# Block 2's shifts and scales as 512-column products with loads of their own and partial sums through DRAM

## The chip, the cores and the metric

The kernel runs on one core of a Trainium2 chip. The time is the device time of one execution in microseconds (us): before the change 2770.35 us, the median of 3 runs (2768.22 to 2776.49). One execution was also taken with the hardware profiler; all rows below are from it. The engines are PE (TensorE; PEld is its weight load), ACT (ScalarE), DVE (VectorE), POOL (GpSimd), and SP (SyncE), which only issues DMAs here.

## The reference, cut to what matters

Two transformer blocks with two layers each run one after the other. Block 1 has 512 rows of width 1024. In each of its layers one projection feeds four kinds of attention: "fox" (causal softmax), stick-breaking, latent (causal softmax again, with low-rank queries and keys), and attention over a memory; a gate and an output projection end the layer. Block 2 modulates its rows by shifts and scales that depend on two condition vectors alone, and so on nothing that block 1 computes:

```python
def adaln(cond, w_mod_l, b_mod_l, n_chunks):
    m = jax.nn.silu(cond) @ w_mod_l[:, :n_chunks * D_MODEL] + b_mod_l[:n_chunks * D_MODEL]
    return jnp.split(m, n_chunks, axis=-1)

def modulate(x, shift, scale):
    return layer_norm(x) * (1 + scale) + shift
# in layer l of block 2, for the latents and for the context:
sh1, sc1, g1, sh2, sc2, g2 = [m[:, None, :] for m in adaln(c, w_mod[l], b_mod[l], N_MOD)]
ctx_mod = adaln(c_ctx, w_mod[l], b_mod[l], 2 if last else N_MOD)
```

The weights of one layer are 1024 rows by 6144 columns of float32, 24 MB, and there are two layers. The left operand has two rows (c and c_ctx).

## The kernel before, in words

`block1` (L600) computes one layer of block 1. In its gaps it runs a generator, `adaln` (L415), which computes the shifts and scales of the same layer of block 2: layer 0's beside layer 0 of block 1, and layer 1's beside layer 1. The generator is put into the list `bg` after the fox attention, and `tick` advances it by one `yield`. There are ticks after the stick-breaking projections, in every second step of stick-breaking attention (L674), after the latent projections, around the latent attention and in the gate's loop; `drain` runs what is left.

One step of `adaln` makes 512 of the 6144 columns. It fetches the 1024 weight rows of these columns in four loads of 512 KB (`wraw`, L318: two times 128 rows by 512 columns). The loads go into the three buffers `w` of a ring that all weights of the two blocks share, and they are issued by SP, whose queue runs in order. For each group of 128 rows, four products of 128 columns each go to the four column tiles of the PE array (32 columns wide), the same left operand `cT` in each, and accumulate over the eight groups in one PSUM tile `pj` (two buffers, which all projections share). So a step is 32 products, and a layer is 12 steps and 48 loads. A float32 product is two PE instructions. DVE adds the bias into the row tile `mr`; when all steps are done, `mr` goes to DRAM (`mod_d`) and comes back in two layouts, to be transposed into `modc` and `modw`.

The names that the change touches: `wraw` and `pj` as above; `copy` (L125) moves a tile on ACT or DVE, taking turns when it isn't told which; `small(..., "ty", bufs=4)` is a tile of 128 by 512 with four buffers, used all over block 1; `causal_attn` (L483) is the fox and the latent attention, eight iterations each; `full_attn` (L505) the memory attention. The order of instructions on each engine is set by a list scheduler at build time, not by the order of the code; at run time each engine takes its list in order.

## Time and profile before

| what | value |
|---|---|
| time of the runs | 2770.35 us (2768.22 to 2776.49) |
| the profiled execution | 2777.7 us, its span 2775.9 us |
| PE busy | 2406.4 us, 87% of the span |
| PE busy from 90 to 400 us (layer 0 of block 1) | 278.84 of 310 us |
| PE busy from 480 to 790 us (layer 1 of block 1) | 278.14 of 310 us |
| loads of `w_mod` | 96 of 512 KB, issued from 90.8 to 747.9 us |

A group's row in the profile gives the engine, the line of the kernel, the operation, the tiles it writes and reads (out<-in), the shape, the count, and busy time; a row of the timeline gives start, length and the same, and in brackets the idle time before it and what ended it. L151 is the helper that issues every product, so products are told apart by their tiles: `pj<-w,cT` are those of `adaln`.

### The profile page before, as it was taken

The page shows a single profiled execution, that of the slowest core. Times are in us where ns is not written, and L with a number is a line of the kernel's source. Part 1 is how long each engine was busy: PE and PEld are TensorE (multiplying, and loading weights), DVE is VectorE, ACT ScalarE, POOL GpSimd, SP SyncE. Part 2 cuts the span into 40 slices and gives each one's busy share as a digit, 9 for nine tenths or more (in the row PEclk, how much of TensorE's full clock was granted, in tenths as well). Part 3 has the DMA queues.
Part 4 walks back from the last instruction along what each step waited for, and adds up shares of the span by engine and source line. Part 5 has one row for each costly group of instructions (what it writes and reads, how often), then busy time and mean ns, then how long its engine had stood idle before and what let it go on. Part 6 is the DMA issues. An engine that isn't in the chain of part 4 may idle for free.

```text
span 2775.9 us, 39464 instructions
## 1 busy us (share of the span) xinstructions
PE 2406.4 (87%) x16255; PEld 1439.1 (52%) x16255; DVE 1224.7 (44%) x2367; ACT 801.2 (29%) x1522; POOL 508.8 (18%) x389
## 2 busy tenths in 40 slices
PE   6988889988998887995999999995798959988887
PEld 5765667655677665774333333334576733333323
DVE  4423554423666977866010101028778661112213
ACT  3353332363334434742101010103337420000001
POOL 3101222011233234042001010104322420000001
PEclk9999999999999997997999999998999969999998
DMA  5353562354444124035899999982221459999996
GB/s 179 116 169 120 164 182 84 107 184 141 133 134 153 61 99 128 8 131 212 355 393 349 419 341 420 340 337 100 68 68 30 160 207 410 421 420 421 421 421 233
DMA packets 216746, 613.17 MB, mean 221 GB/s; under 512 B 37592, under 2 KB 110830, under 8 KB 170486
## 3 DMA queue, kind: packets, MB, share of 16 engines
q1 hardware_dynamic: 207142, 576.74, 55.8%
q0 software_dynamic: 5440, 20.45, 2.6%
q10 hardware_dynamic: 3984, 13.45, 1.2%
q8 instruction: 128, 2.10, 0.3%
q14 instruction: 52, 0.43, 0.0%
HBM read 581.92 MB, written 28.67 MB: 220 GB/s over the span
## 4 chain that ended last, share of the span: by engine, by line
PE 35%; DVE 13%; DMA 11%; issue 8%; ACT 2%; POOL 2%; DVEq 0%; POOLq 0%; ACTq 0%; SPq 0%
PE pm L151 20%; PE pj L151 5%; PE pa L151 5%; DMA w<-in_w_up_dram 4%; DMA w<-in_w_gate_dram 4%; DVE acc L865 3%; DMA w<-in_w_down_dram 2%; PE pt L151 2%; PE pt L160 1%; DVE wl L331 1%; PE ptm L160 1%; DVE s L245 1%; POOL lnst L249 1%; ACT P L471 1%; DVE ng L468 1%
## 5 line engine op out<-in xcount | busy, mean ns | idle before, releaser
L151 PE MATMUL pm<-w,q 128*64 128x512 f32 (+1 forms) x1600 | 359.5, 597 | 40.3 <-DMA w<-in_w_up_dram 27.6
L151 PE MATMUL pm<-w,xT 128*32 128x512 f32 x3072 | 338.7, 599 | 0.0
L151 PEld LDWEIGHTS pm<-w,q 128*64 128x64 f32 x1600 | 122.6, 141 | 265.3 <-issue 200.5
L329 ACT ACTIVATE wh<-w 128x1024 fp32r<-128x1024 f32 (+2 forms) x154 | 161.3, 1050 | 317.2 <-PE pj L151 106.7
L331 POOL TENSOR_TENSOR wl<-w,wh 128x1024 fp32r<-128x1024 f32 (+1 forms) x57 | 143.5, 2520 | 464.0 <-ACT wh L329 448.0
L151 PE MATMUL pj<-hTh,wh 128*128 128x512 f32 x512 | 215.8, 422 | 13.3 <-ACT ty L301 7.2
L151 PEld LDWEIGHTS pm<-w,xT 128*32 128x32 f32 x3072 | 104.4, 111 | 228.1 <-issue 223.6
L151 PE MATMUL pj<-hTl,wh 128*128 128x512 f32 x512 | 207.7, 406 | 0.0
L151 PE MATMUL pj<-hTh,wl 128*128 128x512 f32 x512 | 206.1, 406 | 0.0
L151 PE MATMUL pm<-w,hid 128*32 128x512 f32 x1536 | 178.5, 593 | 0.0
L331 DVE TENSOR_TENSOR wl<-w,wh 128x1024 fp32r<-128x1024 f32 (+2 forms) x97 | 132.4, 1366 | 102.7 <-ACT wh L329 102.1
L1276 DVE TENSOR_TENSOR q<-pm,q 128x512 f32<-128x512 f32 x24 | 16.6, 692 | 285.6 <-PE pm L151 285.6
L160 PE MATMUL pt<-ident,P 128*128 128x128 f32 x712 | 121.2, 290 | 13.0 <-DVE mx L133 4.8
L151 PE MATMUL pa<-wh,hTh 128*128 128x512 f32 x256 | 106.3, 416 | 22.4 <-DVE ty L963 15.1
L1276 DVE TENSOR_TENSOR ty<-pm,ty 128x512 f32<-128x512 f32 x16 | 11.1, 691 | 256.4 <-PE pm L151 256.4
L151 PEld LDWEIGHTS pj<-hTh,wh 128*128 128x128 f32 x512 | 100.7, 197 | 40.5 <-issue 8.9
L1180 POOL DMA_INDIRECT q<-rowsl,idx x16 | 15.4, 960 | 563.0 <-PE ptm L160 432.7
L151 PEld LDWEIGHTS pj<-hTh,wl 128*128 128x128 f32 x512 | 99.5, 194 | 26.0 <-issue 3.3
L151 PEld LDWEIGHTS pj<-hTl,wh 128*128 128x128 f32 x512 | 100.2, 196 | 24.7 <-issue 4.2
L468 DVE TENSOR_REDUCE ng<-pa 128x1 f32<-128x513 f32 (+5 forms) x124 | 93.4, 756 | 35.1 <-PE pa L151 33.1
L151 PEld LDWEIGHTS pm<-w,hid 128*32 128x32 f32 x1536 | 50.4, 110 | 112.5 <-issue 110.7
L865 DVE SCALAR_TENSOR_TENSOR acc<-glu,vec,acc 128x512 f32<-128x512 f32 x120 | 108.6, 946 | 0.1
(447 smaller groups left out, 4465.3 us busy)
## 6 DMA issues: line engine op xcount, KB each, us to landing
w<-in_w_gate_dram SPq DMA_DIRECT2D x128, 1024.0 KB
w<-in_w_up_dram SPq DMA_DIRECT2D x127, 1024.0 KB
w<-in_w_down_dram SPq DMA_DIRECT2D x118, 1024.0 KB
w<-in_w_mod_dram SPq DMA_DIRECT2D x96, 512.0 KB
w<-in_w_in_dram SPq DMA_DIRECT2D x94, 512.0 KB
w<-in_w_out_dram SPq DMA_DIRECT2D x40, 512.0 KB
w<-in_w_down_dram SPq DMA_DIRECT2D x16, 512.0 KB
z<-q ACTq DMA_DIRECT2D x8, 512.0 KB
```

The source lines that it names most:

```text
L151: return T.matmul(o, l, r, start=start, stop=stop_, skip_group_check=True, **kw)
L160: T.transpose(o, i, ident[: i.shape[0], : i.shape[0]])
L245: pin(V.bn_stats(s6[:, c, :], x[:, c * w:c * w + w]))
L249: pin(G.tensor_tensor(out=rs, in0=ve, in1=mhalf[:, :n], op=OP.pow))
L329: A.activation(hi, w, AF.Copy)
L331: (lo_eng or (G if lot[0] % 3 == 0 else V)).tensor_tensor(out=lo, in0=w, in1=hi.bitcast(F32), op=OP.subtract)
L468: V.tensor_reduce(ng, S_[:, :, lo:hi], axis=AX, op=OP.max, negate=True)
L471: A.activation(P[:, i, lo:hi], S_[:, i, lo:hi], AF.Exp, bias=ng[:, i:i + 1], accum_out=su[:, i:i + 1])
L865: V.scalar_tensor_tensor(acc[:, c, :n], glu[:, c, tap:tap + n], w, acc[:, c, :n], op0=OP.mult, op1=OP.add)
L1180: pin(G.indirect_dma_start(out=r, out_offset=None, in_=s["rows"][:], in_offset=bass.IndirectOffsetOnAxis(ap=s["idx"][:, i:i + 1], axis=0)) ...
L1276: V.tensor_tensor(out=x, in0=up[b][h], in1=x, op=OP.mult)
```

## The change

A step now makes half of the sum for 512 columns: it takes 512 of the 1024 rows as four groups of 128, and gives each group to one of the four column tiles, as one product of 512 columns. Each column tile has a group of its own, nothing is accumulated, and the four partial sums stand in partitions 0, 32, 64 and 96 of `pj`. A step has 4 products and 2 loads, and a layer has 24 steps. The loads go into two buffers `wm` of the generator's own pool, and a step issues those of the next one, so the weights of the other projections have the ring to themselves. `copy` brings the whole tile of partial sums to a `ty` tile, a DMA issued by ACT writes it to DRAM (`part_d`), and when all steps are done, the partial sums come back as a tile of 96 by 8 by 128, DVE adds the eight, and the bias. Ticks are added: in every step of stick-breaking attention, and in every iteration of `causal_attn`.

```diff
     def adaln(l, pool):
-        mr = pool.tile([128, 12, 128], F32, tag="mr", name="mr")
...
-        for u in range(12):
+        part_d = dr.tile([2, 128, 6 * D], F32, name=f"adp{l}")
+        def wm():
+            return pool.tile([128, 1024], F32, tag="wm", name="wm", bufs=2)
+        def load(n):
+            u, h = divmod(n, 2)
+            ws = []
+            for j in range(2):
+                w = wm().rearrange("p (k c) -> p k c", k=2)
+                nc.sync.dma_start(w, a["w_mod_2"][l, 512 * h + 256 * j:512 * h + 256 * j + 256,
+                                                  512 * u:512 * u + 512].rearrange("(k p) c -> p k c", p=128))
+                ws.append(w)
+            return ws
+        ws = load(0)
+        yield
+        for n in range(24):
+            u, h = divmod(n, 2)
             p = pj()
-            for kq in range(4):
-                w = wraw(a["w_mod_2"][l], 2 * kq, 2, 512 * u, 512)
-                for k in range(2):
-                    for g in range(4):
-                        mm(p[32 * g:32 * g + 32, :128], cT[:, 2 * kq + k, :], w[:, k, 128 * g:128 * g + 128],
-                           kq == 0 and k == 0, kq == 3 and k == 1, tile_position=(0, 32 * g))
-            V.tensor_tensor(out=mr[:, u, :], in0=p[:, :128], in1=mr[:, u, :], op=OP.add)
+            for g in range(4):
+                mm(p[32 * g:32 * g + 32, :], cT[:, 4 * h + g, :], ws[g // 2][:, g % 2, :], True, True,
+                   tile_position=(0, 32 * g))
+            if n < 23:
+                ws = load(n + 1)
+            y = small([128, S], "ty", bufs=4)
+            copy(y, p)
+            nc.scalar.dma_start(part_d[h, :, 512 * u:512 * u + 512], y)
             yield
-        for g in range(4):
-            nc.sync.dma_start(mod_d[l]..., mr[32 * g:32 * g + 2, :, :])
...
+        m8 = wm()[:96].rearrange("p (a b) -> p a b", b=128)
+        for h in range(2):
+            nc.sync.dma_start(m8[:, 4 * h:4 * h + 4, :], ...part_d[h]...)
+        m9 = wm()
...
+        for w_ in (4, 2, 1):
+            V.tensor_tensor(out=m8[:, :w_, :], in0=m8[:, :w_, :], in1=m8[:, w_:2 * w_, :], op=OP.add)
+        mraw = m9[:96, 128:256]
+        V.tensor_tensor(out=mraw, in0=m8[:, 0, :], in1=m9[:96, 0:128], op=OP.add)
+        nc.sync.dma_start(mod_d[l].rearrange("c (k p) -> (c k) p", p=128), mraw)
...
 # causal_attn, end of each iteration
+                tick(1)
 # stick-breaking attention
-                if j % 2 == 0:
-                    tick(1)
+                tick(1)
```

SP's queue beside stick-breaking attention and the latent projections of layer 0, before (`w` is a buffer of the shared ring; `wk` and `wq` are the latent up-projections' weights):

```order
L321 DMA w<-in_w_in_dram 128x4x256 x2
L321 DMA w<-in_w_mod_dram 128x2x512
L694 DMA P<-in_k_tabs_dram 128x1024
L321 DMA w<-in_w_mod_dram 128x2x512 x3
L749 DMA wk<-in_w_mla_kv_up_dram 128x4x64 x2
```

and now (`wm` are the two own buffers):

```order
L428 DMA wm<-in_w_mod_dram 128x2x512 x2
L321 DMA w<-in_w_in_dram 128x4x256 x2
L428 DMA wm<-in_w_mod_dram 128x2x512 x2
L773 DMA wk<-in_w_mla_kv_up_dram 128x4x64 x2
L428 DMA wm<-in_w_mod_dram 128x2x512 x16
L718 DMA P<-in_k_tabs_dram 128x1024
```

Sixteen loads of `wm`, those of eight steps, now stand behind each other, and the last two of them are those of the step that PE takes after the latent projections; `wk` has moved ahead of them.

PE in the latent attention of layer 0 (`pa<-q,q` are scores, `pt<-ident,P` transposes of the probabilities, `pt<-P,v` products with the values), before:

```order
L151 MATMUL pj<-w,cT 32x128 x8
L160 MATMUL pt<-ident,P 128x128 x4
L151 MATMUL pj<-w,cT 32x128 x16
L151 MATMUL pt<-P,v 64x128 x4
L151 MATMUL pa<-q_2193,q_2195 128x128
```

and now, at the same place:

```order
L160 MATMUL pt<-ident,P 128x128 x2
L151 MATMUL pj<-wm,cT 32x512 x2
L160 MATMUL pt<-ident,P 128x128 x2
L151 MATMUL pj<-wm,cT 32x512 x2
L151 MATMUL pt<-P,v 64x128 x4
L151 MATMUL pa<-q_1988,q_1990 128x128
```

The four products of a step mostly stand as two pairs, one for each load, with other work between; before, the products of one load were eight, and those of two or more loads often stood together.

ACT at the same place, before (`P,su<-pa,ng` are the exponentials):

```order
L471 ACTIVATE P,su_2403<-pa,ng_2401 128x512 x2
L329 ACTIVATE wh<-w 128x1024
L131 ACTIVATE P<-pt 128x512
L471 ACTIVATE P,su_2441<-pa,ng_2439 128x128 x2
L329 ACTIVATE wh<-w 128x1024
```

and now:

```order
L495 ACTIVATE P,su_2204<-pa,ng_2202 128x512 x2
L131 ACTIVATE ty<-pj 128x512
L445 DMA adp_1142<-ty 128x512
L131 ACTIVATE P<-pt 128x512
L495 ACTIVATE P,su_2254<-pa,ng_2252 128x128 x2
```

The casts of the gate's weights (`wh<-w`) have moved behind this place, and in each iteration a copy of partial sums and the issue of its DMA stand in ACT's list between the exponentials.

## Rows read from the trace of the kernel before

**Rows 1.** The page, part 1: busy time and share of the span.

```profile
PE 2406.4 (87%) x16255; PEld 1439.1 (52%) x16255; DVE 1224.7 (44%) x2367; ACT 801.2 (29%) x1522; POOL 508.8 (18%) x389
```

**Rows 2.** The chain of waits from 780 to 830 us: its earliest two pieces.

```profile
822.99 0.04 issue
823.03 7.05 PE pj L151 x58
```

**Rows 3.** PE's waits in 0 to 460, 171 to 232, 565 to 600, 460 to 860 us.

```profile
PE pj L151 <- DMA w<-in_w_mod_dram: 16.7, 12, 3.3
...
PE pj L151 <- DMA w<-in_w_mod_dram: 8.2, 7, 2.8
...
PE pj L151 <- DMA w<-in_w_mod_dram: 8.7, 7, 2.3
...
PE pj L151 <- DMA w<-in_w_mod_dram: 18.3, 13, 2.8
```

**Rows 4.** The timeline of PE: 32 instructions of `adaln`, and what starts behind them.

```profile
281.40 1.08 PE L151 MATMUL pj<-w,cT 128*32 128x128 f32 x32
282.41 0.91 PE L151 MATMUL pa<-q,q 96*128 96x384 f32 x2
```

**Rows 5.** The page, part 5: 512-column products in two and in four column tiles.

```profile
L151 PE MATMUL pm<-w,q 128*64 128x512 f32 (+1 forms) x1600 | 359.5, 597 | 40.3 <-DMA w<-in_w_up_dram 27.6
L151 PE MATMUL pm<-w,xT 128*32 128x512 f32 x3072 | 338.7, 599 | 0.0
```

**Rows 6.** The timeline of SP and PE: issues of loads, and the products that waited for them.

```profile
260.37 0.37 SPq L321 DMA_DIRECT2D w<-in_w_mod_dram  x1
...
264.92 0.64 PE L151 MATMUL pj<-w,cT 128*32 128x128 f32 x16 [3.20 <-DMA w<-in_w_mod_dram]
265.98 2.08 PE L151 MATMUL pj<-cqk,wk 128*128 128x512 f32 x2 [0.41 <-DVE mr L430]
...
270.10 1.02 PE L151 MATMUL pj<-cqk,wk 128*128 128x512 f32 x2
...
282.10 0.88 SPq L321 DMA_DIRECT2D w<-in_w_mod_dram  x2
...
286.30 0.64 PE L151 MATMUL pj<-w,cT 128*32 128x128 f32 x16 [1.22 <-DMA w<-in_w_mod_dram]
...
657.05 0.65 PE L151 MATMUL pj<-w,cT 128*32 128x128 f32 x16 [2.47 <-DMA w<-in_w_mod_dram]
658.11 2.08 PE L151 MATMUL pj<-cqk,wk 128*128 128x512 f32 x2 [0.41 <-DVE mr L430]
```

**Rows 7.** Windows: busy time of the engines, granted clock (PEclk), DMA share, GB/s.

```profile
180.00:190.00 10.00, 6.91 (x69) 3.58 (x65) 1.85 (x3) 4.18 (x5) 0.00 (x0) 0.68 0.76 250
```

**Rows 8.** The timeline of PE: first scores of latent attention, first output product, both layers.

```profile
279.60 0.39 PE L151 MATMUL pa<-q,q 96*128 96x128 f32 x2
...
388.25 0.50 PE L151 MATMUL pa<-wh,hTh 128*128 128x512 f32 x1 [0.25 <-ACT hTh L369]
...
671.93 0.39 PE L151 MATMUL pa<-q,q 96*128 96x128 f32 x2
...
785.67 0.50 PE L151 MATMUL pa<-wh,hTh 128*128 128x512 f32 x1 [0.36 <-ACT hTh L369]
```

**Rows 9.** The timeline of ACT and DVE, and ACT's issues of a 512 KB write.

```profile
259.01 0.60 ACT L131 ACTIVATE q<-pj 128x512 f32<-128x512 f32 x1 [10.13 <-PE pj L151]
...
197.46 0.69 DVE L133 COPY mx<-pt 128x512 f32<-128x512 f32 x1 [2.81 <-PE pt L151]
...
L565 ACTq DMA_DIRECT2D z<-q x4: 326/329/336, 14.4 to 21.0; - x4
```

**Rows 10.** The timeline of PE and SP: late gate weights, and the end of layer 0.

```profile
356.12 0.50 PE L151 MATMUL pj<-hTh,wh 128*128 128x512 f32 x1 [2.03 <-ACT wh L329]
...
384.97 0.97 SPq L1522 DMA_DIRECT2D natr<-P  x1
...
413.12 0.80 PE L151 MATMUL pa<-wh,hTh 128*128 128x512 f32 x1 [4.62 <-DVE q L825]
```

More of the change, by code (lines that the diff above doesn't have):

```diff
@@ L432, in adaln @@
-        for g in range(4):
-            nc.sync.dma_start(mod_d[l].rearrange("c (u g j) -> c u g j", g=4, j=128)[:, :, g, :],
-                              mr[32 * g:32 * g + 2, :, :])
-        mraw = small([96, 128], "mraw", bufs=1)
-        nc.sync.dma_start(mraw, mod_d[l].rearrange("c (k p) -> (c k) p", p=128))
+        part_d = dr.tile([2, 128, 6 * D], F32, name=f"adp{l}")
[10 more added lines that the diff above has]
+            return ws
@@ new lines, in adaln @@
+        m8 = wm()[:96].rearrange("p (a b) -> p a b", b=128)
+        for h in range(2):
+            src = part_d[h, 0:1, 0:128]
+            nc.sync.dma_start(m8[:, 4 * h:4 * h + 4, :],
+                              bass.AP(src.tensor, src.offset, [[128, 96], [32 * 6 * D, 4], [1, 128]]))
+        m9 = wm()
+        for c in range(2):
+            nc.sync.dma_start(m9[48 * c:48 * c + 48, 0:128], a["b_mod_2"][l].rearrange("(k p) -> k p", p=128))
+        yield
+        for w_ in (4, 2, 1):
+            V.tensor_tensor(out=m8[:, :w_, :], in0=m8[:, :w_, :], in1=m8[:, w_:2 * w_, :], op=OP.add)
@@ L443, in adaln @@
                 V.tensor_scalar(modc[l][:, s0:s0 + 8], modc[l][:, s0:s0 + 8], 1.0, None, op0=OP.add)
-        mrow = mr[0:4, 0:8, :].rearrange("p a b -> p (a b)")
+        mrow = wm()[0:4, :]
         for c in range(2):
```

3 lines of the change are left out of this document (removed).

## The prediction

> **What bounds the kernel now.** I read the busy times first: PE is busy for 87% of the span, no other engine for half of it [rows 1]. Then the chain of waits, which follows the end of the run back to 823 us and no further [rows 2]. The generator's work lies ahead of that, from 90 to 760 us, so no row says directly what a microsecond saved there is worth. I go by PE's own account: in the two layers of block 1 PE is busy for nine tenths of the time, and what follows it needs the layer's output, so time given back to PE there shortens the run, unless attention's chain (scores, maximum, exponential, transpose, values) is what PE was waiting for. The waits name one cause above the others: the generator's own loads, 16.7 us in layer 0 and 18.3 us in layer 1 [rows 3]. Then the timeline for prices, and the order of the changed kernel for places.
>
> **The price of a step.** Before, 32 instructions, the products of two loads, keep PE for 1.01 us, from 281.40 to the next start at 282.41 [rows 4]: 0.505 us for a load. A 512-column instruction costs 338.7/3072 = 0.110 us when four column tiles work side by side, and 359.5/1600 = 0.225 us with two [rows 5]. So a step that stands together (8 instructions) takes 0.88 us, and a pair that stands alone (4) takes 0.90 us: the pair fills half the array for as long as the step would have filled all of it. In PE's order the 48 steps stand in 77 separate groups, 39 in layer 0 and 38 in layer 1. At 0.89 us they take 68.5 us, where 96 loads at 0.505 took 48.5 us. That is 20 us more of PE, not less, and where it stands decides.
>
> **Part by part, both layers together.**
>
> *Up to the latent attention:* 64 of the 96 loads are used there before and 32.3 us of products; now 33 groups, 29.4 us. That is -2.9 us.
>
> *The head of the latent stage:* PE waits 3.20 us and 2.47 us there for a load that was issued 4.55 us earlier (260.37 to 264.92), and the products behind each wait take 2.08 us a pair, where the same pair takes 1.02 us at 270.10 [rows 6]: PE's lower clock level, 1.2 GHz, after the idle time. Now that step's two loads are the last of the sixteen in SP's queue and go out as the tiles of the step before come free, with the latent projections, over a hundred products, still between. So these waits go, and the slow products: 3.20 + 2.47 + 2 x 1.06 = -7.8 us. If the lower clock stays for another reason, it is -5.7.
>
> *Stick-breaking attention:* 16 loads a layer on either side. Before, waits of 8.2 and 8.7 us [rows 3], and in layer 0 a stretch of 10 us at a mean clock of 0.68 [rows 7], which is 6.4 us at half speed and 3.2 us of work lost: 20.1 us. After, a buffer's next load goes out when its pair is done; from issue to product takes 4.2 us (282.10 to 286.30) to 4.55 us [rows 6], and with the pair's 0.9 us a step can't follow its predecessor within 5.1 to 5.5 us. Eight such steps are 42 us. The scheduler moved the stick-breaking projections ahead of this stretch, so less covers the waits than before. The bounds: all waits gone, -20 us; or they stay, with as much lower clock again in both layers, +15. I take the nearest row: seven waits of 1.2 us on average, five to six a layer, no long idle: 14 us against 20.1, so -6 us.
>
> *Latent attention to the output projection:* 32 loads before, 16.2 us; now 44 groups, 39.2 us: 23 us more if nothing covers them, with as many waits as before. From below: this stage takes 108.6 us in layer 0 and 113.7 in layer 1 [rows 8]. I stepped through the new order by hand, each load 4.4 us after its issue: 54 us until the generator's pairs are nearly used up (9 us of them waits), 31 us with the first half of the gate's 192 products, 22.5 with the other half, 107.5 us a layer, since half of the gate now stands alone after attention. That would be -7 us, the late gate weights gone with it (2.03 us [rows 10]). But the hand count leaves out what ACT and DVE cost attention, and here every step puts on ACT a copy, 0.60 us, and an issue, 0.33 us [rows 9], in front of an exponential; when the pair's load is late, ACT waits too, and behind it the next iteration. Between -7 and +23 I take +9.
>
> *ACT and DVE elsewhere:* 48 copies of 0.60 or 0.69 us replace 24 short additions, and 48 issues of 0.33 us come on top, some 40 us on two engines [rows 9]. Outside attention ACT and DVE have room, and I cost them at nothing; if ACT sets the pace of stick-breaking, four copies and eight issues are 5 us a layer, which is inside that part's upper bound.
>
> *The ends:* the partial sums make one more round trip through DRAM. In layer 0 other products follow. In layer 1 about 61 output products (14 us) stand ahead of the transposes, and 18 ahead of the second ones: 0 to 5 us, I take +2. At the end of layer 0 a 3.8 MB copy (`natr`) goes out and PE later waits 4.62 us [rows 10]; now it goes out sooner, ahead of the last step's loads and not behind them. Nothing either way, bounds -5 and +5.
>
> The sum: -2.9 - 7.8 - 6 + 9 + 2 = -5.7 us. Against the profiled 2777.7 us that is 2772; that execution lies 7.4 us above the median, so against the median of 2770.35 it is 2764.7, say 2765 us.
>
> **The rivals.**
>
> *Slower: the two buffers set the pace of attention.* In the latent and the memory attention nine steps follow each other, and a step needs 5.1 to 5.5 us for its loads alone. If an iteration's own chain is that long too, each late pair holds PE, the copy behind it holds ACT, and the exponentials behind that are late: the 23 us of pairs are then fully on the path, and stick-breaking is at +5. -2.9 - 7.8 + 5 + 23 + 2 = +19, and with 10 us of lower clock from the new gaps 2800 us. It decides once a load takes over 5 us to land. For it: these loads share the DMA engines with 48 new writes, and 0.76 of the engines' time is taken in 180 to 190 us [rows 7]. Against it: at most two loads are in flight, where three or four bunched before. A rule that would push the same way: the Trainium skill (TensorEngine Tiling (Array Packing), Key Properties) says that a change of tiling mode drains TensorE. That would add to each of the 77 groups. The trace doesn't show it: the next full-width product starts 1.01 us after the first of the 32, before their last record ends at 1.08 us [rows 4]. By the rule the price would be an estimated 0.16 us (the 0.60 us of a record less 4 x 0.110 of streaming) twice a group, 25 us; I give it nothing of its own.
>
> *Faster: the loads stop being waited for.* All 35 us of waits [rows 3] go with the 5 us of lower clock behind them, the pairs fall into gaps that attention leaves anyway, and the gate's weights come early: -2.9 - 7.8 - 20 - 5 = -36, 2735 us. For it: the order gives most pairs a place behind other work. Against it: two buffers instead of three, and a step of two loads can't be fetched before the one ahead of it is used. The Trainium skill (TensorEngine Tiling (Array Packing), Instruction Overhead) puts some 60 cycles on each matmul; with 1152 instructions fewer that is an estimated 29 us at 2.4 GHz in favour of the long products. The rows disagree: 31.6 ns for a 128-column instruction against 110/4 = 27.5 for the same columns of a long one is 4 ns, 6 us in all, and it is in the sum.
>
> **How the numbers follow.** The forecast has 0.5, its own range 2748 to 2778. The slower rival has 0.3 and the faster one 0.2. A difference of less than 0.3%, 8.3 us, can't be told from no change here. Of the forecast's half, 0.23 lies below 2762, 0.25 within, and 0.02 above; of the slower rival 0.29 above and 0.01 within; of the faster 0.19 below and 0.01 within. Together 0.42 faster, 0.27 the same, 0.31 slower. The range 2736 to 2800 leaves out 0.1 on each side.
>
> **What would show it.** The products `pj<-wm,cT` should come to 0.9 us a group, 4 instructions or 8; a pair at 0.45 would break the price. At the first product with `wk` of the latent stage there should be no wait of over a microsecond ahead and no 2.08 us pair. Waits for `w_mod` loads should be many and short, 1 to 2 us, most of them inside attention, 25 to 45 us in all; under 15 us the faster rival is right. From the first latent scores to the first output product should take 108 to 118 us a layer; at 125 the slower one is. The forecast is wrong as a whole if the time changes outside block 1, where the order of instructions is the same as before.

## The result, and the profile after

The changed kernel takes 2819.3 us (2814.73 to 2820.95, 4 runs) beside 2771.7 us for the kernel before on the same chip: 1.0169 times as long, 95% interval 1.0155 to 1.0183, some 47 us slower. The forecast was 2765 us, with 2736 to 2800 as its range. The profiled execution has a span of 2819.0 us, against 2775.9.

The first part of the page after, and its row for the generator's products, answer to [rows 1]:

```profile
PE 2432.3 (86%) x15103; PEld 1413.4 (50%) x15103; DVE 1233.6 (44%) x2375; ACT 821.9 (29%) x1546; POOL 500.9 (18%) x387
...
L151 PE MATMUL pj<-wm,cT 128*32 128x512 f32 x384 | 94.6, 666 | 41.1 <-DMA wm<-in_w_mod_dram 40.3
```

PE is busy for 25.9 us more (2406.4 before) and idle for 17.2 us more. So neither busy time nor idle time alone is the answer.

The landmarks after, which answer to [rows 8] (timeline of PE, both layers):

```profile
280.75 0.39 PE L151 MATMUL pa<-q,q 96*128 96x128 f32 x2
...
409.62 0.79 PE L151 MATMUL pa<-wh,hTh 128*128 128x512 f32 x1 [3.47 <-ACT hTh L369]
...
697.02 0.39 PE L151 MATMUL pa<-q,q 96*128 96x128 f32 x2
...
820.33 0.50 PE L151 MATMUL pa<-wh,hTh 128*128 128x512 f32 x1 [0.97 <-ACT hTh L369]
```

From the first latent scores to the first output product it is 128.9 and 123.3 us, where it was 108.7 and 113.7. The stretch alone misleads, since part of the gate now lies in it that lay elsewhere. So I cut each layer at its landmarks and split each part in three. A layer's stretch begins at the first product of the forget gate's sums (`pj<-cst,lf`), is cut at the first latent scores, and ends with the last output product (`pa<-wh,hTl`). These are the windows, with the columns of [rows 7] (busy time of the engines, PEclk, DMA share, GB/s). Before: layer 0 up to the latent attention and from there to the last output product, then layer 1:

```profile
66.02:279.60 213.58, 190.89 (x1433) 137.03 (x1433) 74.22 (x147) 93.14 (x169) 24.81 (x34) 0.96 0.43 135
279.60:441.12 161.52, 147.08 (x948) 107.28 (x947) 85.40 (x157) 51.50 (x122) 38.12 (x20) 0.96 0.51 154
487.94:671.93 183.99, 166.40 (x1229) 111.45 (x1229) 61.61 (x127) 82.13 (x148) 23.26 (x32) 0.97 0.43 134
671.93:859.48 187.55, 171.09 (x1134) 130.40 (x1133) 103.93 (x181) 65.53 (x146) 46.51 (x20) 0.95 0.45 144
```

After, the same four, and stick-breaking attention of layer 1 by itself (548.48 to 653.97 before, at a clock of 0.98):

```profile
63.04:280.75 217.71, 195.43 (x1009) 126.41 (x1009) 79.16 (x147) 100.43 (x179) 29.49 (x36) 0.94 0.43 129
280.75:458.89 178.14, 161.31 (x796) 105.01 (x795) 88.98 (x161) 54.85 (x124) 31.70 (x17) 0.94 0.60 181
505.67:697.02 191.35, 169.75 (x805) 102.20 (x805) 63.30 (x126) 86.55 (x155) 23.10 (x33) 0.92 0.41 121
697.02:902.92 205.90, 181.03 (x982) 126.48 (x981) 99.51 (x184) 68.37 (x148) 43.92 (x19) 0.96 0.51 160
570.18:681.80 111.62, 93.87 (x408) 52.88 (x407) 28.34 (x61) 60.09 (x95) 18.11 (x30) 0.86 0.43 129
```

The reader sees the parts grow by 4.1, 16.6, 7.4 and 18.4 us, the clock fall in the parts up to the latent attention, and the DMA share rise in those behind it. For the account below I took such windows of 4 us each: what PE's clock took away is busy time times (1 - PEclk), *work* is the busy time without that, *idle* is what is left. Both layers together, before to after:

| part | length | work | lost to the clock | idle |
|---|---|---|---|---|
| up to the latent attention | 397.6 to 409.1 | 344.9 to 341.6 | 12.3 to 23.6 | 40.3 to 44.0 |
| of it stick-breaking | 215.6 to 216.9 | 180.5 to 161.0 | 5.8 to 20.4 | 29.2 to 35.5 |
| of it the head of the latent stage | 36.5 to 31.9 | 24.9 to 24.1 | 3.2 to 1.6 | 8.4 to 6.3 |
| latent attention to the last output product | 349.2 to 384.0 | 304.4 to 327.9 | 13.8 to 14.4 | 30.9 to 41.6 |
| both, with 46.8 us between the layers | 793.5 to 839.9 | 687.7 to 708.0 | 28.5 to 40.3 | 77.2 to 91.6 |

So +46.4 us is 20.3 of work, 11.8 of lower clock and 14.4 of idle time. The span grew by 43.1 us, since the stretch begins 3.0 us earlier after the change (63.04 against 66.02). What lies behind block 1 didn't change.

The timeline of PE after shows the single cases:

```profile
263.09 1.07 PE L151 MATMUL pj<-wm,cT 128*32 128x512 f32 x8 [0.36 <-ACT q L131]
264.09 0.61 PE L160 MATMUL pj<-ident,kr 128*32 128x128 f32 x4
265.00 1.13 PE L151 MATMUL pj<-cqk,wk 128*128 128x512 f32 x2 [0.30 <-DVE ty L133]
...
287.84 1.05 PE L151 MATMUL pj<-wm,cT 128*32 128x512 f32 x4 [1.65 <-DMA wm<-in_w_mod_dram]
288.82 0.43 PE L151 MATMUL pt<-P,v 128*64 128x128 f32 x2
...
298.81 1.05 PE L151 MATMUL pj<-wm,cT 128*32 128x512 f32 x4 [2.67 <-DMA wm<-in_w_mod_dram]
...
615.64 1.92 PE L151 MATMUL pj<-wm,cT 128*32 128x512 f32 x4 [4.01 <-DMA wm<-in_w_mod_dram]
```

A whole half step (8 instructions) keeps PE for 1.00 us to the next start, and a pair alone (4) for 0.98: the pair costs as much as the whole. At the head of the latent stage [rows 6] the wait and the slow products are gone. At 615.64 PE waited 4.01 us, and the pair behind it took 1.92 us, nearly twice as long; in the window around it the granted clock was 0.67:

```profile
610.00:620.00 10.00, 5.99 (x20) 1.67 (x13) 2.34 (x3) 3.75 (x4) 0.00 (x0) 0.67 0.52 159
```

The latent part has one more wait, which isn't the generator's load. PE after, SP after, and SP before:

```profile
854.23 1.12 PE L160 MATMUL pj<-ident,c 128*128 128x128 f32 x4 [7.39 <-ACT c L259]
...
836.22 0.54 SPq L471 DMA_DIRECT2D wm<-mod  x2
837.98 0.39 SPq L321 DMA_DIRECT2D w<-in_w_in_dram  x1
838.43 4.67 SPq L1503 DMA_DIRECT2D c<-in_ctx_dram  x2
...
782.74 2.94 SPq L1479 DMA_DIRECT2D c<-in_ctx_dram  x2
```

The rows of block 2's context (`c`) are loaded by SP too, and after the change their loads stand behind the partial sums' round trip through DRAM, 56 us later than before. PE waits 7.4 us for them late in layer 1; before, it didn't wait there. That is 7.4 of the 10.7 us of idle time that the latent part gained. Of the kernels below, e2, e7 and e14 have no such wait, e8 has one of 8.2 us for the round trip itself, e16 has 10.0, and the others 5.9 to 7.4 us.

### The profile page after: what moved, and what is told of

The parts are those of the page before. It is cut to its first block, busy times and chain, and to the rows that moved or that the text cites. A ratio compares the mean times of both kernels' runs of the same rounds, so it can differ in the third digit from the quotient of the medians.

```text
span 2819.0 us, 37307 instructions
## 1 busy us (share of the span) xinstructions
PE 2432.3 (86%) x15103; PEld 1413.4 (50%) x15103; DVE 1233.6 (44%) x2375; ACT 821.9 (29%) x1546; POOL 500.9 (18%) x387
## 4 chain that ended last, share of the span: by engine, by line
PE 53%; DMA 18%; DVE 14%; issue 8%; ACT 4%; POOL 2%; SPq 0%; ACTq 0%; DVEq 0%; POOLq 0%
PE pj L151 19%; PE pm L151 17%; PE pa L151 10%; DMA w<-in_w_up_dram 5%; DMA w<-in_w_gate_dram 4%; DMA w<-in_w_down_dram 4%; PE pt L151 3%; DMA wm<-in_w_mod_dram 3%; DVE acc L889 3%; PE pt L160 2%; DVE wl L331 1%; DMA w<-in_w_in_dram 1%; DVE P L135 1%; DVE s L245 1%; PE ptm L160 1%
## 5 line engine op out<-in xcount | busy, mean ns | idle before, releaser
L1300 DVE TENSOR_TENSOR q<-pm,q 128x512 f32<-128x512 f32 x24 | 16.6, 692 | 285.4 <-PE pm L151 285.4
L151 PE MATMUL pj<-wm,cT 128*32 128x512 f32 x384 | 94.6, 666 | 41.1 <-DMA wm<-in_w_mod_dram 40.3
L151 PE MATMUL pa<-wh,hTh 128*128 128x512 f32 x256 | 105.5, 413 | 21.6 <-DVE ty L987 15.1
L151 PEld LDWEIGHTS pj<-hTh,wh 128*128 128x128 f32 x512 | 99.6, 195 | 38.9 <-issue 10.1
L160 PEld LDWEIGHTS pt<-ident,P 128*128 128x128 f32 x712 | 80.7, 144 | 58.7 <-issue 31.0
```

The source lines that it names most:

```text
L151: return T.matmul(o, l, r, start=start, stop=stop_, skip_group_check=True, **kw)
L160: T.transpose(o, i, ident[: i.shape[0], : i.shape[0]])
L1300: V.tensor_tensor(out=x, in0=up[b][h], in1=x, op=OP.mult)
```

## The experiments

The theories after the result: *shape* (a pair of long products fills half the array for a whole step's time), *placement* (the added ticks), *buffers* (two own buffers make each load follow the products before it), *ACT* or *copies* (the copy stands between the exponentials), and, from the second round on, *writes* (256 KB of partial sums for each half step disturb the loads). All numbers at once; the ratio is to the kernel before on the same chip, and work, clock and idle are of the stretch of the table above:

| kernel | us | ratio (95%) | work | clock | idle |
|---|---|---|---|---|---|
| before | 2771.7 | 1 | 687.7 | 28.5 | 77.2 |
| after | 2819.3 | 1.0169 (1.0155 to 1.0183) | 708.0 | 40.3 | 91.6 |
| e1 old ticks | 2854.7 | 1.0316 (1.0288 to 1.0344) | 713.9 | 44.4 | 117.6 |
| e2 before, new ticks | 2771.5 | 1.0015 (1.0004 to 1.0026) | 688.4 | 27.4 | 80.4 |
| e3 short products | 2778.9 | 1.0039 (1.0023 to 1.0056) | 689.6 | 25.8 | 87.5 |
| e4 ring loads | 2794.5 | 1.0086 (1.0059 to 1.0112) | 710.0 | 19.9 | 82.7 |
| e5 full array | 2813.8 | 1.0174 (1.0141 to 1.0206) | 685.8 | 42.8 | 109.5 |
| e6 narrow copy | 2788.4 | 1.0072 (1.0044 to 1.0099) | 711.9 | 16.5 | 77.7 |
| e7 before, 256 columns | 2769.4 | 1.0004 (0.9990 to 1.0019) | 687.3 | 27.4 | 85.1 |
| e8 stick ticks | 2776.6 | 1.0027 (1.0009 to 1.0046) | 686.7 | 27.9 | 81.2 |
| e9 narrow write | 2787.2 | 1.0068 (1.0046 to 1.0089) | 712.8 | 20.2 | 80.0 |
| e10 mixed loads | 2774.1 | 1.0018 (1.0000 to 1.0036) | 689.7 | 28.6 | 74.1 |
| e11 DVE copies | 2830.4 | 1.0214 (1.0181 to 1.0248) | 713.5 | 31.8 | 103.2 |
| e12 ring, 256 columns | 2821.3 | 1.0188 (1.0157 to 1.0219) | 687.8 | 40.2 | 112.4 |
| e13 linear write | 2798.3 | 1.0112 (1.0084 to 1.0140) | 685.3 | 31.3 | 99.4 |
| e14 ring, narrow write | 2772.7 | 1.0016 (0.9996 to 1.0035) | 707.9 | 15.1 | 67.3 |
| e15 short, wide write | 2805.9 | 1.0137 (1.0113 to 1.0162) | 690.1 | 37.3 | 98.1 |
| e16 ring, linear write | 2786.1 | 1.0062 (1.0044 to 1.0079) | 683.8 | 30.4 | 92.0 |
| e17 ring, two rows | 2792.0 | 1.0085 (1.0067 to 1.0102) | 708.6 | 29.2 | 85.3 |
| e18 ring, 256, two rows | 2767.4 | 1.0003 (0.9990 to 1.0015) | 684.6 | 24.6 | 83.4 |

Every kernel is scheduled anew, so an edit also moves instructions that it doesn't name; kernels with the same products differ by 3 to 6 us in work. What such a new order is worth by itself was not measured. The medians are from different chips and rounds, in which those of the kernel before lie between 2767.2 and 2771.7, so a difference of two rows is good to some 4 us.

**e1, the ticks of before in the changed kernel.**

```diff
-            yield
+            if h:
+                yield
 # causal_attn
-                tick(1)
 # stick-breaking attention
-                tick(1)
+                if j % 2 == 0:
+                    tick(1)
```

> The changed kernel with the ticks where they were before (none in causal_attn, every second step of stick-breaking), and one yield for two half steps: long products, two own buffers, copies and sums through DRAM stay. Placement theory (the added ticks push half of the gate out of attention and leave PE idle in stick-breaking at a lower clock): most of the 47.6 us goes, 2775 to 2790, and PE's windows in 150 to 215 us show the granted clock of before. Shape theory (a pair of 512-column products takes 0.9 us for half a step, 20 us of PE, wherever it stands): 2800 to 2820. Buffer theory (two buffers set the pace): each late load still holds PE, 2800 to 2815, waits for w_mod 40 us or more.

2854.7 us, 35 us slower than the changed kernel, which no theory expected. Without the added ticks a step is two rounds of the two buffers in one place, and idle time is 26 us longer. It isn't longer waits for the loads: they are 35.7 us here and 40.3 in the changed kernel. Why this kernel is so much slower stays open; the added ticks help the change.

**e2, the new ticks in the kernel before.**

```diff
-        for u in range(12):
+        for n in range(24):
+            u, h = divmod(n, 2)
...
-            for kq in range(4):
+            for kq in (2 * h, 2 * h + 1):
...
+                tick(1)              # causal_attn, and each step of stick-breaking
```

> The kernel before (128-column products, loads in the shared ring, bias added into the row tile) with the added ticks and half steps: one step is 16 products and two loads, and DVE adds each half sum. Placement theory: this alone costs 30 to 45 us, 2800 to 2815, with the latent to output stretch at 120 to 129 us a layer. Shape theory and buffer theory: within 8 us of before, 2764 to 2780.

1.0015: 4 us, 7 at most by the interval. The stretch of 130.7 us from the latent scores to the output product in layer 0 came too (as with the change), and cost nothing by itself. Placement falls, and with it the sign that I had given for the slower rival, "at 125".

**e3, short products in the changed kernel.**

```diff
-            for g in range(4):
-                mm(p[32 * g:32 * g + 32, :], cT[:, 4 * h + g, :], ws[g // 2][:, g % 2, :], True, True, ...)
+            for k in range(4):
+                for g in range(4):
+                    mm(p[32 * g:32 * g + 32, :128], cT[:, 4 * h + k, :], ws[k // 2][:, k % 2, 128 * g:128 * g + 128], k == 0, k == 3, ...)
...
-            copy(y, p)
+            copy(y, p[:, :128])
```

> The changed kernel (own two buffers, added ticks, copy to ty, sums through DRAM) with 128-column products as before: a half step is 16 products that accumulate over its four groups of rows, the copy is 128 columns and the write 64 KB. Shape theory: the 20 us of half-filled array, the longer copies and the larger writes go, 2785 to 2800. Placement theory: stays at 2805 to 2820. Buffer theory: the waits for the loads are still there, 2805 to 2820.

2778.9: 40 us of the 47 are gone, and work is back at 689.6. But the edit also makes copies and writes a quarter as wide, so it doesn't say which of these it was.

**e4, the loads in the shared ring.**

```diff
-                w = wm().rearrange("p (k c) -> p k c", k=2)
-                nc.sync.dma_start(w, ...)
-                ws.append(w)
+                ws.append(wraw(a["w_mod_2"][l], 4 * h + 2 * j, 2, 512 * u, 512))
...
-        ws = load(0)
...
+            ws = load(n)
...
-            if n < 23:
-                ws = load(n + 1)
```

> The changed kernel with the loads of w_mod in the shared ring of three buffers, fetched at the step that uses them, as before; long products, added ticks and sums through DRAM stay. Buffer theory: 20 us or more goes, under 2800, and waits for w_mod fall below 25 us. Shape and placement theory: 2810 to 2825.

2794.5, 25 us less, with the work of the changed kernel; clock and idle fall by 29 us. PE's waits, from 60 to 920 us, of this kernel and then of the changed one:

```profile
PE pa L151 <- ACT hTh L369: 17.1, 2, 13.0
PE pj L151 <- DMA w<-in_w_mod_dram: 12.3, 14, 2.3
```

```profile
PE pj L151 <- DMA wm<-in_w_mod_dram: 40.3, 27, 4.0
```

The loads' waits fall to a third; a part of that comes back as a wait for `hTh` at the first output product. The buffer theory holds for this pair of kernels. The loads themselves don't land sooner: by their end records, 16 for each load, the median from issue to landing is 4.8 us here and 4.5 in the changed kernel. What the ring gives is that a load is issued longer before it is needed.

**e5, the array filled for each load.** Four products of 256 columns a load, two groups of rows by two halves of the columns:

```diff
-            for g in range(4):
-                mm(p[32 * g:32 * g + 32, :], cT[:, 4 * h + g, :], ws[g // 2][:, g % 2, :], True, True, ...)
+            for j in range(2):
+                for g in range(4):
+                    mm(p[32 * g:32 * g + 32, :256], cT[:, 4 * h + 2 * j + g // 2, :],
+                       ws[j][:, g // 2, 256 * (g % 2):256 * (g % 2) + 256], j == 0, j == 1, ...)
...
-            nc.scalar.dma_start(part_d[h, :, 512 * u:512 * u + 512], y)
+            nc.scalar.dma_start(part_d[h, :, u].rearrange("k c p j -> k (c p) j"), y)
```

> The changed kernel with each load's 256 rows by 512 columns taken as four products of 256 columns, two groups of rows by two halves of the columns, so that the products of one load fill all four column tiles; the two loads of a half step accumulate, and the copy is 256 columns. Own buffers, added ticks and sums through DRAM stay, and PE's order has 78 groups against 77. Shape theory (a late load leaves a pair alone, which fills half the array for 0.9 us): a group of four takes 0.45 us, PE's busy time falls by 20 us or more, and the time falls to 2775 to 2790, as with the 128-column products (2779). Instruction-length theory (long float32 products cost more than their columns wherever they stand): 2800 or more. Copy theory (ACT's copy and the write between the exponentials): half of its cost goes, about 2800.

Work falls by 22 us, as shape says, and the time by 5.5 by the medians and not at all by the ratios (1.0174 and 1.0169): idle time takes the rest. Shape alone isn't the answer either.

**e6 and e9, narrow copies, and wide copies with narrow writes.**

```diff
 # e6
-            copy(y, p)
-            nc.scalar.dma_start(part_d[h, :, 512 * u:512 * u + 512], y)
+            copy(y, p[:, :128])
+            nc.scalar.dma_start(part_d[h, :, 512 * u:512 * u + 128], y)
 # e9
+            copy(y, p)
+            nc.scalar.dma_start(part_d[h, :, 512 * u:512 * u + 128], y[:, :128])
```

> The changed kernel with its long products in pairs, but only 128 of the 512 columns of each partial sum are copied and written (the rest of the sums is left out, and the reading back takes one block for all). Shape theory: the time stays at 2805 to 2825. Copy theory (copies of 0.6 us and writes of 256 KB hold attention and the loads): 2775 to 2795. If both have a part, about 2800.

> The changed kernel with its copies of 512 columns, but only 128 columns of each tile of partial sums are written to DRAM (64 KB a step, the rest is left out as with the narrow copies). Write theory (the 256 KB writes delay the loads that the two buffers wait for): as the narrow copies, 2785 to 2797, and the loads land 0.5 us sooner than in the changed kernel. Copy theory (ACT's 0.6 us between the exponentials): 2810 to 2822.

2788.4 and 2787.2: the width of the copy on ACT costs nothing that can be seen, and with the 192 KB that e9 doesn't write go 32 us (28 by the ratios). Issues and their median time to landing, of the changed kernel, then of e9:

```profile
wm<-in_w_mod_dram SPq DMA_DIRECT2D x96, 512.0 KB, 4.8
...
adp<-ty ACTq DMA_DIRECT2D x48, 256.0 KB, 4.2
```

```profile
wm<-in_w_mod_dram SPq DMA_DIRECT2D x96, 512.0 KB, 4.3
...
adp<-ty ACTq DMA_DIRECT2D x48, 64.0 KB, 3.4
```

The page's medians go by the loads whose landing it could pair with their issue, 24 of the 96 after and 23 in e9. By the end records of all 96 it is 4.5 and 4.2 us, and 4.2 in the kernel before: the wide writes make a load land 0.3 us later. If each of the 48 half steps followed the one before by its loads, that would be an estimated 14 us, half of what went. How the writes cost the rest isn't shown. PE's waits for the loads fall by 10.1 us (40.3 to 30.2), the loss to its lower clock falls by 20.1 us, and work is 4.8 us more.

**e7 and e8, variants of the kernel before.** e7 has e5's products with the ring, old ticks and whole steps; e8 is e2 without the ticks in `causal_attn`.

```diff
 # e7
-            V.tensor_tensor(out=mr[:, u, :], in0=p[:, :128], in1=mr[:, u, :], op=OP.add)
+            copy(y, p[:, :256])
+            nc.scalar.dma_start(part_d[:, u].rearrange("k c p j -> k (c p) j"), y)
 # e8, causal_attn of e2
-                tick(1)
```

> The kernel before (shared ring, old ticks, whole steps of four loads) with 256-column products, four a load in the four column tiles, and one copy and one write of 256 columns a step instead of the addition, the sums through DRAM at the end. By the prices of the rows (4 ns for each 128-column instruction above its columns) PE has 6 us less: 2760 to 2768. If sums through DRAM or the copies cost something by themselves: 2772 to 2785.

> The kernel before with half steps and the added ticks in stick-breaking alone, none in causal_attn, so that the generator's last half steps stand behind attention. If the ticks in causal_attn are what covers the loads, this is slower than the kernel with all added ticks (2771): 2775 to 2790. If they only move the gate out of attention, it is faster: 2755 to 2767.

2769.4 and 2776.6. In e7, 768 instructions fewer leave the work at 687.3, so the 6 us that I expected from them aren't there (the account of the prediction below says why), and the sums through DRAM, written 24 times, cost nothing that can be told. Fewer ticks are no better than more.

**e10, more prefetch for the short products**: a half step's first load goes to an own buffer, a step ahead, its second to the ring.

```diff
-            if n < 23:
-                ws = load(n + 1)
+            if n < 23:
+                own.append(load(n + 1, 0))
+            ws = own.pop(0) + load(n, 1)
...
+                if j:
+                    ws.append(wraw(a["w_mod_2"][l], 4 * h + 2, 2, 512 * u, 512))
```

> The kernel with short products and added ticks (2779), where of a half step's two loads the first goes to the two own buffers, issued a step ahead, and the second to the shared ring. Prefetch theory (two buffers make each load follow the products before it, and the waits of some 34 us are what is left to win): waits for w_mod fall under 20 us and the time to 2750 to 2764, faster than before. If the waits only hide idle time that comes back elsewhere (in stick-breaking's chain, or behind attention): 2765 to 2780.

2774.1. The waits for loads go from 33.9 to 5.7 us, and the idle time only from 87.5 to 74.1. PE's waits of e10:

```profile
PE pa L151 <- ACT P L703: 22.0, 11, 4.6
PE pt L160 <- DVE P L135: 12.1, 8, 2.2
...
PE pj L151 <- DMA wm<-in_w_mod_dram: 5.7, 4, 1.8
```

PE now waits for the exponentials of stick-breaking (3.1 us in the kernel before) and for the scaling of the probabilities (1.8 us). This fits a floor that attention's own chain sets under the loads, and would explain why none of these kernels beats the kernel before; it is argued and not shown. In e10 the wait for the context rows (5.9 us) comes on top, which the kernel before doesn't have and which could be moved away; no run tried it.

**e11, copies on DVE, writes issued by POOL.**

```diff
-            copy(y, p)
-            nc.scalar.dma_start(...)
+            copy(y, p, eng="v")
+            nc.gpsimd.dma_start(...)
```

> The changed kernel with all copies of partial sums on DVE and their writes issued by POOL, so that ACT's list has neither between the exponentials; all else as it was. ACT theory (a late load holds the copy, and behind it ACT's exponentials): 2785 to 2800. If any engine of attention's chain that holds the copy does the same, or the copies aren't the matter: 2808 to 2825.

2830.4, slower. PE's wait for DVE's scaling of the probabilities is 18.7 us here and 6.4 in the changed kernel. The theory that the copy's place on ACT is what costs falls; the expectation's other case, that any engine of attention's chain which holds the copy does the same, fits.

**e12, ring and 256 columns**: the edits of e4 and e5 together.

```diff
+                ws.append(wraw(a["w_mod_2"][l], 4 * h + 2 * j, 2, 512 * u, 512))
...
+                    mm(p[32 * g:32 * g + 32, :256], cT[:, 4 * h + 2 * j + g // 2, :], ...)
```

> The changed kernel with loads in the shared ring and with products of 256 columns that fill all four column tiles for every load; added ticks, half steps, copies of 256 columns and sums through DRAM stay. By the account of the runs so far the work of PE falls by 22 us against the ring with long products (2794), and idle time and lower clock stay at some 100 us in the two layers: 2765 to 2775. If idle time comes back as it did with two own buffers (full array): 2785 to 2795.

2821.3, a miss: 22 us less work than e4, and 27 us more time. What e5 and e12 share is the write in two blocks of 64 partitions, so it became the suspect.

**e13 and e16, the same bytes written as one block**, in e5 and in e12:

```diff
-            nc.scalar.dma_start(part_d[h, :, u].rearrange("k c p j -> k (c p) j"), y)
+            nc.scalar.dma_start(part_d[h, u], y)
```

> The full-array kernel (2814) with its 128 KB of partial sums a step written to one contiguous block, 1 KB for each partition, in place of two blocks of 64 partitions; read back as rows of 256. If the split writes (issued in 0.50 us against 0.33) made its idle time, the work of before and the floor of idle time give 2770 to 2785. If two own buffers and a write of more than 64 KB cost it whatever the pattern, 2800 or more.

> The shared ring, products of 256 columns that fill the array, added ticks, and contiguous writes of 128 KB. If the split writes were the cause of the ring's 2821: 2765 to 2778, that is no faster than before by more than can be told, since attention's own idle time stays. If not: 2805 to 2825.

2798.3 (16 us less than e5) and 2786.1 (35 less than e12). ACT's issue of the write, here in e5 and then in e13 (least, median, most):

```profile
L446 ACTq DMA_DIRECT2D adp<-ty x48: 489/500/601, 138.5 to 821.6; - x48
```

```profile
L446 ACTq DMA_DIRECT2D adp<-ty x48: 326/326/399, 140.4 to 801.3; - x48
```

The pattern of a write matters, by more than 48 x 0.17 us of issuing. The trace shows where they differ. The queue of the writes in e12 and then in e16 (packets, MB, share of 16 DMA engines):

```profile
q10 hardware_dynamic: 10224, 19.74, 1.8%
```

```profile
q10 hardware_dynamic: 10896, 19.75, 1.8%
```

The bytes are the same, and e12 has 14 packets fewer for each of the 48 writes: a write ends with 3 end records and not with 16. Its 128 packets of 1 KB run at most 3 at a time and take 5.5 us, where the write in one block has up to 13 at a time and takes 1.6 us. By these counts the split write goes through 2 of the 16 DMA engines. It lands 10.7 us after its issue at the median (4.4 in e16), the loads land in 6.1 us (4.7 in e16), and PE waits for them:

```profile
PE pj L151 <- DMA w<-in_w_mod_dram: 43.4, 37, 7.0
```

```profile
PE pj L151 <- DMA w<-in_w_mod_dram: 19.6, 15, 2.6
```

These waits are 23.8 us apart, of the 35. In e5 and e13 the same split write lands in 7.0 and 4.1 us, and the waits for loads are 44.1 and 38.7. e7's 24 writes are split as well, 6.6 us each, and cost nothing that can be told there.

**e14, ring and narrow write together**: the edits of e4 and e9.

```diff
+                ws.append(wraw(a["w_mod_2"][l], 4 * h + 2 * j, 2, 512 * u, 512))
...
+            nc.scalar.dma_start(part_d[h, :, 512 * u:512 * u + 128], y[:, :128])
```

> The ring with long products (2794), where only 128 of 512 columns of the partial sums are written, the rest left out. If ring and narrow write take the same idle time away (the loads come early enough either way, and what is left is attention's own chain): 2783 to 2794. If they add up: 2755 to 2770.

2772.7, the kernel before plus nothing that can be told, with work still at 707.9. Neither bound was right: ring (-25) and write (-32) give -47 together, more than either, less than both. But 7.4 of the 47 are neither's: what e14 reads back needs only the first block of columns, so SP issues it at 145.83 and not at the layer's end, and the wait for the context rows is gone. Here the long products' 20 us of work lie where PE would be idle: clock and idle are 82.4 us, the least of all.

**e15, wide writes with short products.**

```diff
-            copy(y, p[:, :128])
-            nc.scalar.dma_start(part_d[h, u], y)
+            copy(y.rearrange("p (a b) -> p a b", b=128), p[:, :128].unsqueeze(1).to_broadcast([128, 4, 128]))
+            nc.scalar.dma_start(part_d[h, :, 512 * u:512 * u + 512], y)
```

> The kernel with short products, own buffers and added ticks (2779), but each copy fills 512 columns (its 128 repeated four times) and 256 KB a step are written, as in the changed kernel. Write theory: 25 to 35 us more, 2800 to 2815. If the wide writes cost only together with the half-filled array: 2775 to 2788.

2805.9, 27 us more than e3: the write theory's range. By the end records loads land in 4.5 us against 4.2, as after and in e9. But PE's waits for the loads are shorter here (30.9 us, 33.9 in e3), so that the time goes by the loads isn't shown. That wide writes go with 22 to 32 us more is repeated in four pairs of kernels (after with e6 and with e9, e3 with e15, e4 with e14, where 7.4 of the 22 are the context rows). Each pair was scheduled anew, and the order of PE's instructions that came out is a rival that no run excludes.

**e17 and e18, only the two used rows written**, in the ring, with long products and with products of 256 columns:

```diff
-            nc.scalar.dma_start(part_d[h, :, 512 * u:512 * u + 512], y)
+            for c in range(2):
+                nc.scalar.dma_start(part_d[c, 4 * h:4 * h + 4, 512 * u:512 * u + 512], y[c::32, :])
```

> The changed kernel with loads in the shared ring, where only the two used rows of each column tile are written (the rows of c and c_ctx, two DMAs of 8 KB for a half step, nothing left out of the result); products of 512 columns, added ticks and copies as in the changed kernel. By the runs so far the wide writes and the own buffers are 45 of the 47.6 us: 2765 to 2775, the same as before. If small writes also give back the rest: under 2762. If two issues on ACT for each half step cost it: 2780 or more.

> As the kernel with two rows written, but with products of 256 columns that fill the array for each load. PE's work falls by 22 us; if idle time and lower clock were only the writes' and the buffers', the time is 2750 to 2760, faster than before. If idle time fills what work leaves, as in the pairs of runs so far (short products own buffers against long ones: 22 us less work, 13 to 16 us more idle): 2762 to 2775.

2792.0 and 2767.4. Between these two the work differs by 24 us and the medians by 24.6: by that, shape is on the path in full here. The account of e17 is from an execution of 2803.5 us, 11 above its median, so its clock and idle are too high for that comparison. e18 mends the change to the time of the kernel before (1.0003), and doesn't beat it. e17 is 19 us slower than e14, which writes 64 KB in one DMA and not 16 KB in two. 7.4 us of that is the wait for the context rows; PE's waits for loads are 25.6 us against 16.4. The rest isn't settled: two issues of 0.48 us on ACT against one of 0.33 are a weak candidate, since e18 has the same two.

## Why the prediction was wrong

Two steps of the prediction failed, and a term that it put at nothing: stick-breaking attention, the latent attention, and the new writes. A chain of kernels gives each edit a price, by the ratios: the ticks and half steps +4 (e2), own buffers and narrow sums through DRAM +7 (e3), 256 KB writes in place of 64 KB +27 (e15), long products in pairs +9 (after). Such a chain adds up to the whole, 47, whatever the causes are, and its shares depend on the order of the steps: with wide writes and long products the ring takes away 23 (e4), with 64 KB writes 14 (e9 to e14, 5.9 of them the wait for the context rows). Of e3's +7, which is several edits at once, 5.9 are the wait for the context rows.

- **The price of a step** came out right in its difference. 77 groups were to cost 20 us more of PE; work rose by 20.3 (20 to 26 in the other kernels with long products), and the kernels that fill the array have 22 to 24 us less. Its two halves were both too low, and that they were so together was luck. A group takes 0.98 to 1.00 us, where 0.89 was predicted, so 77 take 76 us and not 68.5. And before, a group has a price of its own beside its columns. PE before, with 48, 32 and 16 instructions of the generator:

```profile
259.66 1.52 PE L151 MATMUL pj<-w,cT 128*32 128x128 f32 x48 [0.35 <-ACT q L131]
261.11 0.61 PE L160 MATMUL pj<-ident,kr 128*32 128x128 f32 x4
...
280.70 0.22 PE L151 MATMUL pa<-causal,identb 128*128 128x128 bf16 x1
280.76 0.65 PE L151 MATMUL pa<-q,q 96*128 96x256 f32 x2
281.25 0.22 PE L151 MATMUL pa<-causal,identb 128*128 128x128 bf16 x1
281.40 1.08 PE L151 MATMUL pj<-w,cT 128*32 128x128 f32 x32
282.41 0.91 PE L151 MATMUL pa<-q,q 96*128 96x384 f32 x2
...
283.92 0.22 PE L151 MATMUL pa<-causal,identb 128*128 128x128 bf16 x1
284.07 0.65 PE L151 MATMUL pj<-w,cT 128*32 128x128 f32 x16
284.64 0.44 PE L160 MATMUL pt<-ident,P 128*128 128x128 f32 x2
```

They keep PE for 1.45, 1.01 and 0.57 us to the next start: 0.44 for each 16, which is 27.3 ns an instruction and just a quarter of 0.110, and 0.14 us once for the group. So before, 96 loads in 74 groups took some 42 + 10 = 52 us, and the difference is 24 by these rows. The 4 ns that the prediction put on each 128-column instruction are this 0.14 spread over 32, which is why e7 with 768 instructions fewer has only 0.4 us less work and not 6. Ahead of such a group the mask product (`pa<-causal,identb`) also keeps PE for 0.15 us, where it takes 0.06 ahead of full-width scores. So a group costs PE about 0.09 us at its head and 0.14 us beyond its columns. The Trainium skill says that a change of tiling mode drains TensorE (TensorEngine Tiling (Array Packing), Key Properties). The trace agrees in direction: these two prices come near the 0.16 us twice a group of the prediction's estimate, whose reading that the trace doesn't show it was wrong. Whether it is the change of mode is not shown: the 0.14 us are there at 261.11 too, where the next product is in column tiles of 32 as well. To give the rule nothing was right all the same, since there were 74 such groups before and there are 77 now. The same page's Instruction Overhead puts about 60 cycles on a matmul. Added to each, that is an estimated 19 us at 2.4 GHz for the 768 instructions that e7 saves. Its work fell by 0.4 us.
- **Up to the latent attention**: -2.9 predicted, and the work there is -3.3.
- **The head of the latent stage**: -7.8 predicted, -4.6 measured. The two long waits went, as did the 2.08 us pairs at the first product with `wk` [rows 6]; in layer 0 a wait of 2.37 us for a copy took a part of the place, at 271 us, and the pair behind it still took 1.91 us.
- **Stick-breaking**: this step failed, and by the most. It said -6 with "no long idle"; lower clock and idle time rose by 20.9 us, beyond the upper bound of +15. The waits for loads were 12.2 and 11.2 us, longest 3.5 and 4.0, against 8.2 and 8.7 [rows 3], and what PE lost to its lower clock went from 5.8 to 20.4 us. The stretch is as long as before (215.6 and 216.9 us) although 19.5 us of work had moved ahead of it. I had seen that a step can't follow its predecessor within 5.1 to 5.5 us, and still took the row nearest to before.
- **Latent attention to the output**: this step failed too. Between -7 and +23 I took +9, and +2 for the ends; it is +34.8 for both. Work rose by 23.5, the upper end, and no idle time was used up by it: that rose by 10.7 more, of which 7.4 are the wait for the context rows. The hand walk's 54 us until the pairs are nearly used up were 68 in layer 0 (280.75 to 348.95). Its 4.4 us from issue to use was right (4.35 at the median there), and waits for loads were 7.5 us, less than its 9. What it lacked was 5.7 us of lower clock, 5.3 us of waits for ACT's exponentials and DVE's scaling, and 4.5 us of work.
- **The ends**: +2 predicted, between 0 and 5. The wait of 4.62 us [rows 10] went and the one of 7.39 us came, +2.8 together: near, and by luck, since the prediction names neither the context rows nor their place in SP's queue.
- **ACT and DVE elsewhere**: costed at nothing, which was right for the copies (e6 against e9) and left out what came with them. The text names "48 new writes" as a reason for the slower rival and gives them no price. Kernels with writes of 256 KB, where 64 KB do, are 22 to 32 us slower, the largest term that the runs give; how they cost it stays open (a load lands 0.3 us later, and the waits for loads don't make up the rest).
- **The rivals.** The slower one had a part of the mechanism: own buffers cost 23 to 25 us with wide writes (e4), and no idle time hid the pairs' work. Its condition, loads of over 5 us, isn't met: 4.5 us at the median of all 96. Its 2800 us was short by the writes and by the lower clock of stick-breaking. What spoke against it, "at most two loads in flight", may be what made it so, since nothing more was fetched ahead; that fits e4, whose loads land no sooner and are waited for less.
- **Where the time changed** was right: in block 1 alone. But PE's idle time was taken for something that loads alone explain; e10 took 28 us of the loads' waits away, and 13 us of idle time went.

## What to carry to other kernels

Split the time of a busy engine into work, lower clock and idle before arguing from waits: work saved can come back as idle time (e5) and work added can vanish in it (e14). Price a new DMA by what it does to the loads that share the engines and are waited for, not by its issue, and write only the rows that are used, in a pattern that many DMA engines share (e16 against e12). When a loop has only as many buffers as a step needs, nothing is fetched ahead, and a late load is a late step (e4). And look in the queue behind a new round trip: what stands there waits for it, as the context rows did.

## What the runs showed of the hardware

The same 128 KB written from 128 partitions took 0.50 us to issue in two blocks of 64 partitions and 0.33 us in one. In two blocks its packets ran at most 3 at a time and landed in 10.7 us at the median (e12), in one block up to 13 at a time and in 4.4 us (e16); the kernels differed by 35 us.

Four 512-column instructions in two column tiles kept PE for 0.98 us, eight in four column tiles for 1.00. A group of 128-column instructions in four column tiles took 27.3 ns for each and 0.14 us once.

A pair of products behind a wait of 4.01 us took 1.92 us where pairs else take 1.05, at a granted clock of 0.67 around it: here the idle gap was paid a second time. It isn't always: before, behind 2.76 us at 691.20 the generator's 16 instructions took 0.57 us as elsewhere, and behind the same 2.76 us at 183.62 the granted clock was 0.61. All lower clock together cost 11.8 us more than before over the two layers.
